# Hybrid decoder layer, float32, one core: projections of the MLP and of the embedding gate as 2x2 block products with seven multiplications

## The chip, the cores and the metric

The kernel runs on one core of a Trainium2 chip. The metric is device time of one execution in microseconds (us); the median of the runs is compared. Its engines are TensorE (PE; its weight loads are listed as PEld), VectorE (DVE), ScalarE (ACT), GpSimd (POOL) and SyncE (SP, which here only issues DMAs).

## The reference, cut to what matters

One layer: four token mixers (S5, forgetting attention, RWKV-7, stick-breaking attention), a gated merge with output projection and layer norm, then the part that is changed. x is 1024 tokens by 1024 channels, all float32.

```python
merged = sum(jax.nn.sigmoid(gates[:, :, n]) * (branches[n] @ w_branch[i, n]) for n in range(4))
h1 = _layer_norm(DEEPNORM_ALPHA * h + merged @ w_out[i], ln1_g[i], ln1_b[i])
up = jnp.square(jax.nn.relu(h1 @ mlp_w1[i]))                 # 1024 x 4096, squared ReLU
ple = jax.nn.sigmoid(h1 @ ple_gate_w[i]) * (p[i] @ ple_w[i]) # gated embedding, p is 1024 x 256
h = _layer_norm(DEEPNORM_ALPHA * h1 + up @ mlp_w2[i] + ple, ln2_g[i], ln2_b[i])
```

(The names `h1`, `up` and `ple` are put in here for the text.)

## The kernel before, in words

Every large product is made of float32r matmuls of 128x128 weights by 128x512 values. For float32 accuracy each operand is split into a high part (ACT casts it) and a low part (DVE or POOL subtracts), and three matmuls take the place of one: high by high, high by low, low by high. A product over 1024 input channels for one 128x512 output is thus 8 x 3 = 24 matmuls in one PSUM bank (`dense`).

The program is written by a planner: `Driver` keeps a model of when each engine and each value is free, Python generators yield at each step, and PE's order is the order in which their matmuls are emitted. On DVE and ACT the instructions are sorted by the start times of that model (end of `body`); SP and POOL issue in the order of emission. The planner has a cost for each instruction (`Timed.cost`, `T.matmul`); it has none for two engines that get in each other's way.

Weights come as 128x512 float32 tiles `wr` (SP), are split into `wh` and `wl`, and wait there for PE (`WStream`). Stages:

- The mixers and the merge, to about 1012 us.
- `out_proj`: eight blocks of 128 tokens, 48 matmuls each. After each block `h1_block` does layer norm on DVE, PE turns the result (8 transposes), ACT writes h1 times alpha into the accumulators `acc` (tiles `mg`), ACT and DVE write the high and low parts `xh`, `xl`.
- `mlp`: four chunks of 1024 hidden channels. For each: eight up products in two token halves (`up`: ACT takes the ReLU out of PSUM, DVE squares, ACT and DVE split into `wo` tiles); then, for three chunks, eight down products (DVE adds each to `acc`). After the first chunk the gate and embedding products (`gated`). The hidden values never leave SBUF.
- The down product of the fourth chunk is done with tokens on the partitions (`begin`, `step`), so that the last layer norm (`finish`) reads PSUM directly.

In matmuls of 128x512: 384 in `out_proj`; 4 x 8 x 2 x 24 = 1536 up; 3 x 8 x 2 x 24 = 1152 down; 8 x 2 x 24 = 384 gate; 8 x 2 x 6 = 96 embedding; 384 in the last part.

Of the kernel before, what the change touches and what calls it, by code (L numbers as in the profile page):

```python
# [16 lines left out]
P = 128  # L17
S = 1024
# [296 lines left out]
def body(ctx, tc, I, O, dbg=None):  # L315
# [1315 lines left out]
    ypool = pool_in(ctx, name="yp", bufs=4)  # L1631
    tpool = pool_in(ctx, name="tp", bufs=2)
# [38 lines left out]
    ws.limit = len(items)  # L1671
# [8 lines left out]
    wo = pool_in(ctx, name="wo", bufs=16)  # L1680
# [10 lines left out]
    def wo_split(i):  # L1691
        p_ = (wot(), wot())
        split(*p_, wraw[i])
        if i == 6:
            ws.gate = len(items) - 7
        if i + 2 < 7:
            wo_load(i + 2)
        return p_
# [30 lines left out]
    def h1_block(tb, xr):  # L1729
# [3 lines left out]
        for d4 in range(2):  # L1733
# [3 lines left out]
            for j in range(4):  # L1737
                i = d4 * 4 + j
                src = o[:, j * P:(j + 1) * P]
                A.copy(xh[i][:, sl], src)  # L1740
                A.activation(out=acc[i][:, sl], in_=src, func=AF.Copy, scale=ALPHA)
            for j in range(4):
                i = d4 * 4 + j
                V.tensor_tensor(out=xl[i][:, sl], in0=o[:, j * P:(j + 1) * P], in1=xh[i][:, sl].bitcast(F32), op=ALU.subtract)
# [17 lines left out]

    def mlp():
        yield from out_proj()
        for c in range(4):
            hid = []

            def up(w, a, b, h, last):
                hs = slice(h * 512, (h + 1) * 512)
                while tdone[0] < 4 * h + 4:  # L1770
                    yield "wait"
                o = yield from dense(w, KT, xh, xl, h * 512, last=last)
                rl = tpool.tile([P, 512], F32, tag="th", name=nm("rl"))
                A.activation(out=rl, in_=o, func=AF.Relu)
                V.tensor_tensor(out=rl, in0=rl, in1=rl, op=ALU.mult)
                split(a[:, hs], b[:, hs], rl)
            if c == 0:
                hid += [(wot(), wot()) for _ in range(2)]
                for h in range(2):
                    for f in range(2):  # L1780
                        yield from up(ws.get(), *hid[f], h, True)
            for f in range(len(hid), 8):
                w = ws.get()
                hid.append((wot(), wot()))
                for h in range(2):
                    yield from up(w, *hid[f], h, h == 1)
            hh, hl = [a for a, _ in hid], [b for _, b in hid]
            if c < 3:
                for dt_ in range(8):
                    w = ws.get()  # L1790
                    for h in range(2):
                        hs = slice(h * 512, (h + 1) * 512)
                        o = yield from dense(w, KT, hh, hl, h * 512, last=h == 1)
                        V.tensor_tensor(out=acc[dt_][:, hs], in0=acc[dt_][:, hs], in1=o, op=ALU.add)
            else:
                ws.gate = len(items)
                w2 = []

                def begin(tb):
                    outs[tb] = [pmm() if (tb * 2 + h) % 8 < 3 else px() for h in range(2)]  # L1800
                    for j in range(8):
                        T.turned(outs[tb][j // 4][:, j % 4 * P:j % 4 * P + P], acc[j][:, tb * P:(tb + 1) * P], j % 4 == 0)

                def step(tb, h, kt):
                    sl, hs = slice(tb * P, (tb + 1) * P), slice(h * 512, (h + 1) * 512)
                    if kt == len(w2):
                        w2.append(ws.dst[ws.get()])
                    for a, b in ((hh, 0), (hh, 1), (hl, 0)):
                        T.matmul(outs[tb][h], lhsT=a[kt][:, sl], rhs=w2[kt][b][:, hs], start=False, stop=kt == 7 and a is hl)
                for tb in range(3):  # L1810
# [121 lines left out]
```

## Time and profile before

| | |
|---|---|
| median of 3 runs | 1927.45 us (1927.32 to 1929.45) |
| the profiled execution | 1929.31 us, span 1927.5 us |
| instructions in the profile | 26665, of them 10035 matmuls |
| busy: PE, PEld, DVE, ACT, POOL | 98%, 80%, 54%, 33%, 5% |
| mean granted clock of TensorE | 0.988 of full speed |
| moved by DMA | 155.62 MB, mean 81 GB/s |

The span is what the profiler saw between the first and the last instruction; 1.8 us of the execution's own time lie around it. A busy PE is a PE with a matmul in its pipeline: matmuls overlap (one lasts about 0.39 us and the next starts 0.23 us after it), so PE's rate is read from starts, not from durations.

### The profile page before, as it was taken

How to read it: one execution, taken by the hardware profiler on the slowest of the kernel's cores; microseconds unless marked ns; L12 is line 12 of the kernel's file. 1: busy time of each engine (PE TensorE's matmuls, PEld its weight loads, DVE VectorE, ACT ScalarE, POOL GpSimd, SP SyncE). 2: the span in 40 equal slices, each digit the busy share in tenths (PEclk: the TensorE clock that was granted, in tenths of full speed). 3: DMA queues.
4: the chain of work that ended last, by engine and by line, in shares of the span. 5: the costliest groups of instructions: out<-in, count | busy, mean ns of one | idle time of the engine just before them, and what ended most of it. 6: DMA issues, size and time to landing. Idle time of an engine off the chain costs nothing.

```text
span 1927.5 us, 26665 instructions
## 1 busy us (share of the span) xinstructions
PE 1889.2 (98%) x10035; PEld 1546.2 (80%) x10035; DVE 1049.2 (54%) x2312; ACT 635.7 (33%) x1324; POOL 95.1 (5%) x151
## 2 busy tenths in 40 slices
PE   8999999999999999999999999999999999999998
PEld 7877777768788877778778888888888888888886
DVE  8775755527786763888686643233333233223454
ACT  5443342225453214555443242122132123113310
POOL 0331111100000000000000000000000000000000
PEclk9999999999999979999999999999999999999999
DMA  6343322215422314122452121121111111111211
GB/s 248 116 123 94 90 75 86 87 55 155 144 62 81 91 49 122 61 62 62 153 161 85 33 66 46 53 68 45 52 49 50 47 53 44 54 45 50 86 68 55
DMA packets 111888, 155.62 MB, mean 81 GB/s; under 512 B 30592, under 2 KB 51360, under 8 KB 111632
## 3 DMA queue, kind: packets, MB, share of 16 engines
q1 hardware_dynamic: 107872, 140.31, 23.3%
q0 software_dynamic: 3888, 13.62, 2.1%
q8 instruction: 79, 1.29, 0.3%
q14 instruction: 49, 0.40, 0.1%
HBM read 127.40 MB, written 26.48 MB: 80 GB/s over the span
## 4 chain that ended last, share of the span: by engine, by line
PE 66%; DVE 5%; DMA 1%; issue 1%; ACT 1%; DVEq 0%; ACTq 0%; SPq 0%
PE mm L325 57%; PE x L325 8%; DVE R L278 2%; PE x L330 2%; DVE W L278 1%; DVE tq L278 1%; DMA wr<-in_w_in_dram 1%; DVE Z L278 0%; ACT W L278 0%; ACT R L278 0%; DVE th L278 0%; DMA th<-scr_g 0%; PE x L335 0%; DMA st<-scr_qk 0%; DVE WR L278 0%
## 5 line engine op out<-in xcount | busy, mean ns | idle before, releaser
L325 PE MATMUL mm<-t,wh 128*128 128x512 f32 x2880 | 906.8, 396 | 3.4 <-ACT th L278 2.2
L325 PEld LDWEIGHTS mm<-t,wh 128*128 128x128 f32 x2880 | 532.9, 189 | 115.3 <-ACT th L278 2.6
L325 PE MATMUL mm<-t,wl 128*128 128x512 f32 x1440 | 563.3, 391 | 0.8 <-DVE wl L278 0.7
L325 PEld LDWEIGHTS mm<-t,wl 128*128 128x128 f32 x1440 | 271.4, 189 | 59.8 <-DVE wl L278 1.6
L278 ACT CAST wh<-wr 128x512 fp32r<-128x512 f32 (+1 forms) x257 | 156.8, 611 | 445.2 <-PE mm L325 410.6
L278 DVE TENSOR_TENSOR wl<-wr,wh 128x512 fp32r<-128x512 f32 (+1 forms) x207 | 138.5, 671 | 268.4 <-ACT wh L278 265.7
L325 PE MATMUL mm<-wo,wh 128*128 128x512 f32 x768 | 236.5, 389 | 0.0
L325 PEld LDWEIGHTS mm<-wo,wh 128*128 128x128 f32 x768 | 144.1, 188 | 30.0
L325 PE MATMUL mm<-wo,wl 128*128 128x512 f32 x384 | 149.4, 389 | 0.0
L278 DVE TENSOR_TENSOR rl<-rl 128x512 f32<-128x512 f32 x64 | 44.1, 688 | 98.2 <-ACT rl L278 98.2
L325 PE MATMUL mm<-wo,t 128*128 128x512 f32 x384 | 89.0, 391 | 0.0
L325 PEld LDWEIGHTS mm<-wo,wl 128*128 128x128 f32 x384 | 72.1, 188 | 14.9
L325 PEld LDWEIGHTS mm<-wo,t 128*128 128x128 f32 x384 | 71.6, 188 | 14.5
L278 POOL TENSOR_TENSOR wl<-wr,wh 128x512 fp32r<-128x512 f32 x50 | 67.1, 1341 | 280.6 <-ACT wh L278 280.4
L278 DVE TENSOR_TENSOR mg<-mg,mm 128x512 f32<-128x512 f32 x48 | 32.8, 683 | 83.3 <-PE mm L325 83.3
L325 PE MATMUL mm<-y,vh 128*128 128x512 f32 x240 | 75.2, 395 | 0.0
L278 ACT ACTIVATE th<-mm 128x512 f32<-128x512 f32 x60 | 36.3, 606 | 111.9 <-PE mm L325 108.7
L278 ACT ACTIVATE rl<-mm 128x512 f32<-128x512 f32 x64 | 38.2, 597 | 105.1 <-PE mm L325 105.1
L278 DVE TENSOR_TENSOR wo<-rl,wo 128x512 fp32r<-128x512 f32 x64 | 44.4, 693 | 43.9 <-ACT wo L278 43.8
L278 DVE SCALAR_TENSOR_TENSOR th<-th,mm 128x512 f32<-128x512 f32 x64 | 43.6, 681 | 33.5 <-PE mm L325 31.7
L278 ACT CAST wo<-rl 128x512 fp32r<-128x512 f32 x64 | 39.7, 621 | 50.9 <-DVE rl L278 50.9
L278 ACT CAST PTh<-x 128x512 fp32r<-128x512 f32 (+1 forms) x96 | 43.0, 483 | 39.8 <-PE x L330 39.2
(339 smaller groups left out, 2483.7 us busy)
## 6 DMA issues: line engine op xcount, KB each, us to landing
wr<-in_mlp_w_dram SPq DMA_DIRECT2D x116, 256.0 KB
wr<-in_w_in_dram SPq DMA_DIRECT2D x110, 256.0 KB
st<-scr_qk SPq DMA_DIRECT2D x56, 128.0 KB
scr_qk<-st SPq DMA_DIRECT2D x20, 256.0 KB
scr_g<-gs SPq DMA_DIRECT2D x20, 256.0 KB
wr<-in_w_branch_dram SPq DMA_DIRECT2D x40, 128.0 KB
th<-scr_g SPq DMA_DIRECT2D x20, 256.0 KB
xr<-in_xT_dram SPq DMA_DIRECT2D x16, 256.0 KB
```

Source lines behind the costliest of these rows:

```text
L278: r = f(*a, **kw)
L325: return nc.tensor.matmul(out, lhsT=lhsT, rhs=rhs, **kw)
L330: return nc.tensor.transpose(out, in_, idn)
```

## The change

The planner's cost of a matmul is altered. The up products, the gate and the first three chunks of the down product are now done in groups. A group multiplies a 256x1024 block of weights by 1024x1024 values, both seen as 2x2 blocks: weights A11..A22 of 128x512, values B11..B22 of 512 channels by 512 tokens. Instead of eight block products there are seven, of 12 matmuls each, with sums of weights (S1 to S4) and of values (T1 to T4). Part of the adding is done by letting a PSUM bank go on accumulating after it was read (`BANKS`).

- POOL makes the four sums of weights per group; ACT and DVE split seven tiles of weights per group into `wp` pairs.
- The values of an up or gate group are made from h1 once (`operands_h1`). The low part of the last of each four tiles is made by POOL, the others by DVE.
- An up group takes its four blocks out of PSUM (three copies on ACT, three additions on DVE), applies squared ReLU, makes T1 to T4 on DVE, and stores seven 128x512 tiles to DRAM (`scr_H`). All 16 up groups and the 4 gate groups come first; then three times four down groups. `operands_hidden` loads the seven value operands of a chunk (28 tiles) and splits them again.
- The fourth chunk's hidden values go to DRAM (`scr_H3`) and come back for the last part.
- The embedding product is done in two halves beside `h1_block`, and stored to DRAM (`scr_B`); the gate groups load it.
- `yp`, `tp` and `wo` are now in a stack of pools, `mid`, that is closed after `out_proj`; pool `sp` (tiles `wp`, `sx`, `sn`) takes its place, and pool `fin` follows `sp` for the last part.

```diff
-            drv.tensor((max(n, 2 * m) if rhs.dtype == F32R else 4 * max(n, m)) / 2380.0, out, [lhsT, rhs], not kw["start"])
+            drv.tensor((max(n + m // 4, 2 * m) if rhs.dtype == F32R else 4 * max(n, m)) / 2400.0, out, [lhsT, rhs], not kw["start"])
...
-                A.copy(xh[i][:, sl], src)
-                A.activation(out=acc[i][:, sl], in_=src, func=AF.Copy, scale=ALPHA)
...
-                V.tensor_tensor(out=xl[i][:, sl], in0=o[:, j * P:(j + 1) * P], in1=xh[i][:, sl].bitcast(F32), op=ALU.subtract)
+                if j % 2:
+                    V.tensor_copy(acc[i][:, sl], o[:, j * P:(j + 1) * P])
+                else:
+                    A.copy(acc[i][:, sl], o[:, j * P:(j + 1) * P])
...
+    B_OPS = ("B11", "B21", "T2", "T1", "T3", "B22", "T4")
+    A_OPS = ("A11", "A12", "S2", "S1", "S3", "S4", "A22")
+    BANKS = "XYXZXZX"
+    NPAIR, NSN = 5, 8
+    GROUPS = [g for c in range(4) for g in (("U", c, 0), ("U", c, 1), ("P", 0, c), ("U", c, 2), ("U", c, 3))]
+    GROUPS += [("D", c, i) for c in range(3) for i in range(4)]
...
+        def paired(g, name, frees):
+            src = raws[g, name]
+            while (1, 5) not in fed_units or live["pair"] >= NPAIR or drv.ready(src) > drv.now:
+                yield None
+            live["pair"] += 1
+            h, l = pair_of(sp().tile([P, 1024], F32R, tag="wp", name=nm("wp"), bufs=NPAIR))
+            split(h, l, src)
...
+            added(g, "S1", r("A21"), r("A22"), ALU.add)
+            added(g, "S2", r("S1"), r("A11"), ALU.subtract)
+            added(g, "S3", r("A11"), r("A21"), ALU.subtract)
+            added(g, "S4", r("A12"), r("S2"), ALU.subtract)
...
+    def operand(ph, n, src):
+        t = operand_tile(n)
+        h, l = pair_of(t)
+        A.copy(h, src)
+        (G if len(phases[ph].get(n, ())) == 3 else V).tensor_tensor(out=l, in0=src, in1=h.bitcast(F32), op=ALU.subtract)
...
+    def operands_hidden(c):
+        jobs = [(n, kt) for n in B_OPS for kt in range(4)]
...
+                while len(loads) < min(len(jobs), k + 4) and live["sn"] < NSN:
+                    m, j = jobs[len(loads)]
+                    loads.append(sn())
+                    SY.dma_start(out=loads[-1], in_=SCR["H"][c * 4 + j, H_ROW[m]])
...
+    def blocks_of(take):
+        kept = {}
+        def ev(n, o):
+            if n in (0, 2, 3):
+                kept[n] = sn()
+                A.copy(kept[n], o)
+            elif n == 6:
+                take("21", o)
+            else:
+                t = kept.pop({1: 0, 4: 3, 5: 2}[n])
+                V.tensor_tensor(out=t, in0=o, in1=t, op=ALU.add)
+                take({1: "11", 4: "22", 5: "12"}[n], t)
...
+    def down_blocks(i):
+        def ev(n, o):
+            a, h = {0: (0, 0), 1: (0, 0), 2: (0, 1), 3: (1, 1), 4: (1, 1), 5: (0, 1), 6: (1, 0)}[n]
+            t = acc[2 * i + a][:, h * 512:(h + 1) * 512]
+            V.tensor_tensor(out=t, in0=t, in1=o, op=ALU.add)
...
+        for n, (bank, a, x) in enumerate(zip(BANKS, A_OPS, B_OPS)):
...
+            for kt in range(4):
...
+                T.matmul(o, lhsT=h[:, ks], rhs=t[:, 0:512], start=new and kt == 0, stop=False, skip_group_check=not new)
+                T.matmul(o, lhsT=h[:, ks], rhs=t[:, 512:1024], start=False, stop=False, skip_group_check=not new)
+                T.matmul(o, lhsT=l[:, ks], rhs=t[:, 0:512], start=False, stop=kt == 3, skip_group_check=not new)
...
+        yield from ple_half(0, stage0)
+        fed_units["half"] = True
+        while tdone[0] < 8:
+            yield "wait"
+        mid.close()
+        late["stack"] = ctx.enter_context(ExitStack())
+        late["sp"] = pool_in(late["stack"], name="sp", bufs=1)
+        drv.add(fetch_raw(), 2)
+        drv.add(make_pairs(), 2)
+        drv.add(operands_h1(), 3)
...
+        yield from ple_half(1, stage1)
...
+        for g, after in zip(GROUPS, GROUPS[1:] + [None]):
+            end = after is None or phase_of(after) != phase_of(g)
+            if end and after is not None:
+                drv.add(operands_hidden(after[1]), 2)
+            yield from group(g, end)
```

How the instructions move, at three places. The first is POOL's program after the output projection. Before, POOL has only DMA issues there (`y` are the rows of x, `t` the parameters of the last norm):

```order
L278 DMA y_11324<-in_x_dram 128x1024
L278 DMA y_11431<-in_x_dram 128x1024
L278 DMA t_16497<-in_ln_g_dram 128x1024
L278 DMA t_16498<-in_ln_b_dram 128x1024
L1928 UNCONDITIONAL_BRANCH
```

Now it goes on like this (`mg` is h1, `sn` the plain sums of values, `t` and `sx` low parts of operands, `ws` sums of weights from `wr`):

```order
L278 TENSOR_TENSOR sn_11673<-mg_4377,sn_11673 128x512
L278 TENSOR_TENSOR sn_11729<-mg_4375,mg_4371 128x512
L278 TENSOR_TENSOR ws_11758<-wr_11657,wr_11691 128x512
L278 TENSOR_TENSOR ws_11762<-wr_11621,wr_11657 128x512
L278 TENSOR_TENSOR ws_11760<-ws_11758,wr_11621 128x512
L278 TENSOR_TENSOR t_11722<-sn_11719,t_11722 128x512
L278 TENSOR_TENSOR t_11725<-sn_11718,t_11725 128x512
L278 TENSOR_TENSOR sn_11719<-mg_4378,sn_11719 128x512
L278 TENSOR_TENSOR ws_11764<-wr_11623,ws_11760 128x512
L278 TENSOR_TENSOR sn_11775<-mg_4376,mg_4372 128x512
```

From the first operand to the last one of h1, `sx_11899`, POOL has 19 such rows; in the whole program 164 more than before, each a tensor_tensor that reads two SBUF tiles.

The second place is ACT between the two halves of the embedding product. Before, ACT's rows after the output projection split weights and h1 (`xh` is `t`), none of them waiting for a pool:

```order
L278 CAST wh_11574<-wr_10640 128x512
L278 CAST wh_11592<-wr_10659 128x512
L278 ACTIVATE rl_11598<-mm_11542 128x512
L278 CAST t_104<-x_11613 128x128
L278 ACTIVATE mg_4368<-x_11613 128x128
```

Now, after the last value of the first half (`pb_11557`), come the first tiles of pool `sp`, `wp_11573`, and between them and `wp_11611`, which the second half's first matmul needs, seven operand casts:

```order
L278 ACTIVATE pb_11557<-mm_11550 128x512
L278 CAST t_11566<-mg_4371 128x512
L278 CAST wp_11573<-wr_11481 128x512
L278 CAST wp_11578<-wr_11525 128x512
L278 CAST t_11583<-mg_4372 128x512
L278 CAST t_11586<-mg_4373 128x512
L278 CAST t_11589<-mg_4374 128x512
L278 CAST t_11592<-mg_4375 128x512
L278 CAST t_11595<-mg_4376 128x512
L278 CAST t_11598<-mg_4377 128x512
L278 CAST t_11601<-mg_4378 128x512
L278 CAST wp_11611<-wr_11569 128x512
```

The store of `pb_11557` to DRAM must have landed before `wp_11573` may be written, since `sp` lies on the memory of `mid`.

The third place is DVE where one down chunk follows another. Before, a down product has two splits of weights and two additions for 48 matmuls:

```order
L278 TENSOR_TENSOR wl_12311<-wr_12182,wh_12310 128x512
L278 TENSOR_TENSOR wl_12329<-wr_12200,wh_12328 128x512
L278 TENSOR_TENSOR mg_4369<-mg_4369,mm_12297 128x512
L278 TENSOR_TENSOR mg_4370<-mg_4370,mm_12335 128x512
L278 TENSOR_TENSOR wl_12375<-wr_12250,wh_12374 128x512
```

Now, in the last group of the first down chunk (`t` are the low parts of the next chunk's operands, `wp` those of weights):

```order
L278 TENSOR_TENSOR mg_4377<-mg_4377,x_15379 128x512
L278 TENSOR_TENSOR wp_15411<-ws_15338,wp_15411 128x512
L278 TENSOR_TENSOR t_15417<-sn_15383,t_15417 128x512
L278 TENSOR_TENSOR t_15425<-sn_15385,t_15425 128x512
L278 TENSOR_TENSOR mg_4377<-mg_4377,x_15404 128x512
L278 TENSOR_TENSOR wp_15434<-wr_15291,wp_15434 128x512
L278 TENSOR_TENSOR t_15437<-sn_15387,t_15437 128x512
L278 TENSOR_TENSOR mg_4377<-mg_4377,x_15379 128x512
L278 TENSOR_TENSOR wp_15463<-wr_15344,wp_15463 128x512
L278 TENSOR_TENSOR t_15466<-sn_15420,t_15466 128x512
```

From `t_15417` to the last of the 28 operands DVE has 42 such rows, 21 operands, 10 splits of weights and 11 additions, and POOL has 15.

## Rows read from the trace of the kernel before

**Rows 1.** The page: span, busy time of each engine, share of the span, instructions.
```profile
span 1927.5 us, 26665 instructions
PE 1889.2 (98%) x10035; PEld 1546.2 (80%) x10035; DVE 1049.2 (54%) x2312; ACT 635.7 (33%) x1324; POOL 95.1 (5%) x151
```
**Rows 2.** The stretches of the program (mixers and merge; output projection; up, gate and down; last part; tail): us, then busy time and instructions of PE, PEld, DVE, ACT, POOL, granted clock, DMA share, GB/s.
```profile
0.00:1012.50 1012.50, 982.43 (x5971) 794.31 (x5972) 694.05 (x1648) 423.57 (x868) 89.16 (x140) 0.98 0.34 104
1012.50:1105.90 93.40, 93.40 (x443) 77.93 (x442) 63.84 (x174) 26.98 (x129) 4.88 (x10) 1.00 0.19 60
1105.90:1824.80 718.90, 718.90 (x3177) 595.34 (x3176) 241.22 (x374) 173.93 (x305) 0.41 (x1) 1.00 0.16 52
1824.80:1919.00 94.20, 94.20 (x449) 78.65 (x447) 45.60 (x106) 10.98 (x22) 0.64 (x2) 1.00 0.21 73
1919.00:1927.50 8.50, 0.29 (x2) 0.00 (x0) 4.50 (x12) 0.20 (x1) 0.00 (x0) 0.77 0.16 62
```
**Rows 3.** PE in order of time at the start of the output projection, and at the end of it: start, us, instruction (merged).
```profile
1012.58 18.53 PE L325 MATMUL mm<-wo,t 128*128 128x512 f32 x81
1030.94 1.03 PE L330 MATMUL x<-cst,y 128*128 128x128 f32 x8
...
1113.36 1.03 PE L330 MATMUL x<-cst,y 128*128 128x128 f32 x8
1114.14 0.71 PE L325 MATMUL mm<-t,wh 128*128 128x512 f32 x2
```
**Rows 4.** Splits of four tiles in a row on ACT and on DVE, at the start of the last part: start, us, instruction, idle time before it and who ended it; and what follows them on ACT.
```profile
1826.99 2.18 ACT L278 CAST t<-wr 128x512 fp32r<-128x512 f32 x4
1832.02 1.24 ACT L278 CAST t<-wr 128x512 fp32r<-128x512 f32 x2 [2.85 <-DMA wr<-in_mlp_w2t_dram]
1834.07 1.26 ACT L278 CAST t<-wr 128x512 fp32r<-128x512 f32 x2 [0.81 <-DMA wr<-in_mlp_w2t_dram]
1836.48 0.62 ACT L278 CAST t<-wr 128x512 fp32r<-128x512 f32 x1 [1.14 <-DMA wr<-in_mlp_w2t_dram]
```
```profile
1827.72 2.49 DVE L278 TENSOR_TENSOR t<-wr,t 128x512 fp32r<-128x512 f32 x4
```
**Rows 5.** POOL's subtractions of 128x512, as a group: shortest, median, longest in ns.
```profile
L278 POOL TENSOR_TENSOR wl<-wr,wh x50: 1263/1290/1785, 46.2 to 394.4; 128x512 fp32r<-128x512 f32 x50
```
**Rows 6.** DVE and POOL at the same time, three places: start, us, instruction.
```profile
189.93 1.27 POOL L278 TENSOR_TENSOR wl<-wr,wh 128x512 fp32r<-128x512 f32 x1 [11.95 <-ACT wh L278]
...
209.05 1.28 POOL L278 TENSOR_TENSOR wl<-wr,wh 128x512 fp32r<-128x512 f32 x1 [11.61 <-ACT wh L278]
...
108.73 1.29 POOL L278 TENSOR_TENSOR wl<-wr,wh 128x512 fp32r<-128x512 f32 x1 [1.04 <-ACT wh L278]
```
```profile
189.68 0.36 DVE L278 TENSOR_TENSOR tp<-L,Tn 128x192 f32<-128x192 f32 x1
190.07 1.33 DVE L278 TENSOR_TENSOR Tn<-Tn,tp 128x192 f32<-128x192 f32 x1
...
208.85 0.27 DVE L278 TENSOR_TENSOR tp<-L,Tn 128x120 f32<-128x120 f32 x1
209.16 1.32 DVE L278 TENSOR_TENSOR Tn<-Tn,tp 128x120 f32<-128x120 f32 x1
...
109.27 0.75 DVE L278 SCALAR_TENSOR_TENSOR xo<-mm,vec,xo 128x511 f32<-128x511 f32 x1 [4.57 <-ACT xo L278]
```
**Rows 7.** The layer norm of the last block of tokens on DVE, first and last row, and what follows it.
```profile
1106.07 0.69 DVE L278 SCALAR_TENSOR_TENSOR y<-y,mm 128x512 f32<-128x512 f32 x1
...
1110.84 1.41 DVE L278 SCALAR_TENSOR_TENSOR y<-y,rs,y 128x512 f32<-128x512 f32 x2
1112.16 1.29 DVE L278 TENSOR_TENSOR wl<-wr,wh 128x512 fp32r<-128x512 f32 x2
```
**Rows 8.** A store from SBUF to DRAM: issues, KB each, median us from issue to landing.
```profile
scr_v<-vs POOLq DMA_DIRECT2D x8, 128.0 KB, 2.0
```
**Rows 9.** Granted clock (after POOL's busy time) around two pauses of PE; columns as in rows 2.
```profile
420.00:425.00 5.00, 3.11 (x16) 2.26 (x14) 3.71 (x8) 2.55 (x5) 0.00 (x0) 1.00 0.15 52
425.00:430.00 5.00, 2.12 (x7) 1.92 (x8) 2.64 (x9) 0.96 (x2) 0.00 (x0) 0.52 0.30 105
430.00:435.00 5.00, 5.00 (x19) 4.04 (x18) 1.38 (x3) 0.00 (x0) 0.50 (x1) 0.80 0.15 52
...
670.00:675.00 5.00, 4.21 (x20) 3.30 (x18) 4.93 (x6) 0.60 (x1) 0.00 (x0) 1.00 0.00 0
675.00:680.00 5.00, 4.41 (x20) 3.51 (x20) 2.33 (x4) 0.00 (x0) 0.00 (x0) 0.77 0.09 26
680.00:685.00 5.00, 5.00 (x17) 3.65 (x17) 1.80 (x3) 1.23 (x2) 0.00 (x0) 0.50 0.00 0
685.00:690.00 5.00, 5.00 (x15) 3.87 (x15) 1.44 (x3) 1.69 (x4) 0.00 (x0) 0.50 0.00 0
690.00:695.00 5.00, 5.00 (x36) 3.96 (x36) 2.69 (x6) 0.35 (x1) 0.00 (x0) 0.86 0.56 135
```
**Rows 10.** A stretch in which the DMA engines were full; columns as in rows 2.
```profile
440.00:445.00 5.00, 5.00 (x23) 4.14 (x23) 3.37 (x6) 3.28 (x7) 0.00 (x0) 1.00 1.01 301
```

More of the change, by code (lines that the diff above doesn't have):

```diff
@@ L1669, in merged @@
                                op1=ALU.subtract)
-    ws.limit = len(items)
+    ws.limit = last0
     fill = merges()
@@ L1694, in wo_split @@
         if i == 6:
-            ws.gate = len(items) - 7
+            ws.gate = last0 - 1
         if i + 2 < 7:
@@ new lines, in drop, with fetch_raw @@
+    def drop(what):
+        live[what] -= 1
+    def fetch_raw():
+        for g in GROUPS:
+            w1, w2 = sources(g)
+            for name, src, c in (("A11", w1, 0), ("A12", w1, 512), ("A21", w2, 0), ("A22", w2, 512)):
+                while live["raw"] >= NRAW or fed_units.get("loads", 0) < 12:
+                    yield None
+                live["raw"] += 1
+                raws[g, name] = t = wpool.tile([P, 512], F32, tag="wr", name=nm("wr"), bufs=NRAW)
+                SY.dma_start(out=t, in_=src[:, c:c + 512])
+        fed[0] = 1
@@ new lines, in operands_hidden @@
+    def operands_hidden(c):
+        jobs = [(n, kt) for n in B_OPS for kt in range(4)]
+        loads = []
+        for k, (n, kt) in enumerate(jobs):
+            while True:
+                while len(loads) < min(len(jobs), k + 4) and live["sn"] < NSN:
+                    m, j = jobs[len(loads)]
+                    loads.append(sn())
+                    SY.dma_start(out=loads[-1], in_=SCR["H"][c * 4 + j, H_ROW[m]])
+                if k < len(loads) and n in freed[c] and drv.ready(loads[k]) <= drv.now:
+                    break
+                yield None
+            yield from operand(c + 1, n, loads[k])
+            drop("sn")
@@ new lines, in ple_half @@
+    def ple_half(h, stage):
+        for dt_ in range(8):
+            k = 2 + dt_ // 2
+            while (h, k) not in fed_units:
+                yield "wait"
+            o = pmm()
+            for kt in range(2):
+                xa, xb = fed_units[h, kt]
+                ks = slice(dt_ % 2 * 256 + kt * P, dt_ % 2 * 256 + kt * P + P)
+                a, b = (x[:, ks] for x in fed_units[h, k])
+                T.matmul(o, lhsT=a, rhs=xa, start=kt == 0, stop=False)
+                T.matmul(o, lhsT=a, rhs=xb, start=False, stop=False)
+                T.matmul(o, lhsT=b, rhs=xa, start=False, stop=kt == 1)
+                yield
+            if dt_ % 2:
+                used_units.add((h, k))
+                if h:
+                    live["pair"] -= 1 + 2 * (dt_ == 7)
+            t, out = stage(dt_)
+            A.activation(out=t, in_=o, func=AF.Copy, scale=0.5)
+            if out is not None:
+                SY.dma_start(out=out[0], in_=out[1])
@@ L1763, in mlp @@
     def mlp():
+        drv.add(ple_feed(), 2)
         yield from out_proj()
[L1765 to L1778, printed above, removed]
[L1779 to L1835 removed]
@@ new lines, in mlp, with begin, step @@
+        late["stack"].close()
+        late["fin"] = pool_in(ctx, name="fin", bufs=1)
+        ws.gate = len(items)
+        hid, w2 = [], []
+        def begin(tb):
+            outs[tb] = [pmm() if (tb * 2 + h) % 8 < 3 else px() for h in range(2)]
+            for j in range(8):
+                T.turned(outs[tb][j // 4][:, j % 4 * P:j % 4 * P + P], acc[j][:, tb * P:(tb + 1) * P], j % 4 == 0)
+        def step(tb, h, kt):
+            sl, hs = slice(tb * P, (tb + 1) * P), slice(h * 512, (h + 1) * 512)
+            if kt == len(w2):
+                hid.append(ws.dst[ws.get()])
+                w2.append(ws.dst[ws.get()])
+            for a, b in ((0, 0), (0, 1), (1, 0)):
+                T.matmul(outs[tb][h], lhsT=hid[kt][a][:, sl], rhs=w2[kt][b][:, hs], start=False, stop=kt == 7 and a == 1)
```

264 lines of the change are left out of this document (225 added, 39 removed).

## The prediction

> **What bounds the kernel now.** I read the page's busy times first, then the windows by stage, then PE in order of time, and last the other engines at the places where the change gives them work. PE is busy for 98% of the span, POOL for 5% [rows 1]. By stage PE idles only in the mixers: 1012.5 − 982.4 = 30 us. From 1012.5 to 1919 it is busy all the time at a granted clock of 1.00 [rows 2]. In the up, gate and down stage, 718.9 us long, DVE is busy for 241 us and POOL for 0.4. So PE's rate is the bound there: 81 matmuls in a row start over 1030.94 − 1012.58 = 18.36 us, 0.2267 us each [rows 3], and the stage's 1536 + 384 + 96 + 1152 = 3168 matmuls times 0.2267 are 718.2 us of its 718.9. A matmul taken away there is time taken away, as long as the others keep up.
>
> **What is removed.** Up, gate and down are 3072 matmuls; 32 groups of 7 products of 12 make 2688. Embedding, output projection and last part keep theirs. 384 × 0.2267 = **−87.0 us**.
>
> **What steady groups add.** A group lasts 84 × 0.2267 = 19.0 us on PE. In an up group DVE has 18 rows. A tensor_tensor of 128x512 takes 1.29 for two [rows 7] and 2.49 for four [rows 4], so 0.60 to 0.62 each; I take 0.61: 11.0 us. POOL has four sums of weights at a median of 1.29 [rows 5], 5.2 us. The two do not run side by side. A DVE op that needs 0.36 takes 1.33 when a POOL op runs, and one of 0.27 takes 1.32: 0.97 and 1.05 lost. One that reads PSUM is not held (0.75 beside POOL) [rows 6]. Four POOL ops at 0.97 add 3.9: 14.9 of 19.0 us. ACT has 11 rows at (2.18 − 0.62) / 3 = 0.52 [rows 4], under 6 us. Cost 0, hidden behind PE; the cover on DVE is 4 us per group.
>
> **The first transition** (t0 is the end of the output projection). Without waits, PE has half an embedding product (48 matmuls, 10.9), 8 transposes (0.8 [rows 3]), the other half (10.9) and six products (16.3) before the seventh product needs the last operand of h1: t0 + 38.9. Now the waits. The last layer norm keeps DVE until 1112.25, t0 + 6.4 [rows 7], and one split of weights queues behind it (t0 + 7.0), where PE has already waited some 1.3 us. The first half then ends at t0 + 13.0, is taken out of PSUM (0.6) and stored, which takes 2.0 [rows 8]: only at some t0 + 16 may the first tile of the new pool be written. ACT then makes ten casts in order (0.52 each) up to `wp_11611`, t0 + 21.2, its low part at t0 + 22; until there the second half cannot start, so PE idles for some 9 us. Meanwhile DVE starts at t0 + 16.5 on the 44 rows that end with the last low part, 44 × 0.61 = 26.8, and meets POOL's 19 rows, 19 × 0.97 = 18.4: t0 + 61.7. Against 38.9 that is **+23**. Bounds: with no loss beside POOL, PE's own 22 + 10.9 + 16.3 = 49.2, so +10; with each POOL row costing its whole 1.29, 67.8, so +29. I take 23, since the loss was measured.
>
> **Three chunk boundaries.** The operands of a chunk need loads of hidden values that earlier products still write or that share slots with them, so DVE's 42 rows (25.6 us) and POOL's 15 must pass within about 13 products, 35.4 us, of which 2.7 go before the first load lands: 32.6. Eleven of the 42 rows add from PSUM and are not held, so of 15 × 0.97 = 14.6 I count 74%, 10.8: 25.6 + 10.8 = 36.4, 4 us late each, **+12** for three. Bounds: 0, if POOL's ops mostly fall on those additions; and 25.6 + 15 × 1.29 = 45.0, 12.3 late each, 37.
>
> **A rule against it.** By the Trainium skill, SBUF — State Buffer, section Who interferes with whom, a DVE instruction with two SBUF inputs and a GpSimd instruction that reads SBUF exclude each other, and the loser waits for the whole instruction. The trace agrees in kind, and that a DVE op with one SBUF input escapes. By that rule a POOL op that comes first costs DVE all its 1.29 instead of 0.97: rival C below.
>
> **The last part.** Its hidden values now come from DRAM, so a step of 18 matmuls (4.08 us) needs four tiles, two before. Four casts are 2.1, and after four ACT waited 2.85 for the next load [rows 4]: 4.9 per step, 0.8 short over eight steps, 6.4 at most from that; loads made ahead cover about half. I take 3, and 1 for the last addition on DVE ahead of the transposes: **+4**, between 1 and 9.
>
> **The clock.** After a pause of a few us the granted clock stood at 0.52 and 0.80 for ten us, and once at 0.50 for over ten us after a pause of 1.4 among small matmuls [rows 9]. The two pauses of the first transition (about 9 us, and the one at the seventh product) may each cost some 2 us beyond their length: **+4**, between 0 and 14 (two times 7: rows 9 show 0.50 for ten us, 5 us lost, and 0.77 and 0.86 in the five before and behind, 2 us).
>
> **The mixers.** The planner's new cost of a matmul reorders PE there without adding any: 0, within ±10, a third of the 30 us of idle time that stands there [rows 2].
>
> **The sum.** −87 + 23 + 12 + 4 + 4 = −44. The profiled execution took 1929.3, so 1885.3; the median lies 1.9 below it: **1884 us**.
>
> **Rivals.**
> - A, the meeting of DVE and POOL costs little: PE's own path of 49 us holds at the first transition (+10), boundaries are free, last part +4, clock +2: −71, 1856. For it: POOL often waits for its own inputs. Against it: both cases in the trace lose nearly the whole op [rows 6]. Chance 0.20.
> - B, slower than before: DVE's queue in order becomes the bound of the steady groups. A product's bank must be read within about one product, 2.72 us, and an addition behind one held op (1.33) and two others (1.2) comes at that edge. Each late reading then stops PE, in 20 up and gate groups. It turns the sign when the 20 groups lose 44 us, 2.2 us each; at 2.5 us each, 20 × 2.5 = 50: 1934. For it: in-order queue, no cost for the two engines' exclusion in the planner. Against it: 15 of 19 us, and even at 0.69 (the longest DVE op of this kind [rows 7]) and 1.29 it is 12.4 + 5.2 = 17.6. Chance 0.08.
> - C, POOL's op costs DVE its full 1.29 everywhere: first transition 29, boundaries 25.6 + 0.74 × 19.4 − 32.6 = 7.3 each, 22 for three; steady groups 16.2, still hidden. −87 + 29 + 22 + 4 + 4 = −28: 1899. For it: with both queues full, every POOL op starts right behind a DVE op. Against it: rows 6 lose 0.3 less. Chance 0.10.
> - D, loads bind at the boundaries: 28 operands and some 8 weights of 256 KB in 35.4 us are 267 GB/s, and the DMA engines were full at 301 [rows 10], while SP issues them in order behind stores. At 8 us more for each boundary, +24: 1908. Chance 0.08.
> - E, the mixers' order costs 15 us: 1899. Chance 0.05.
> - That the change doesn't do what it says: PE's program has 384 matmuls fewer, of the same shape. The gain could only vanish if they started every 0.259 us (0.2267 × 3072 / 2688) instead of 0.2267; nothing in their form says so. That way lies in B.
>
> **How the numbers follow.** The forecast has 0.49. It and A span 1856 to 1899; the bounds of the first transition (10 and 29), the boundaries (0 and 37) and the clock could add, best to −87 + 10 + 0 + 1 + 0 = −76, 1851. With C, D and E on the upper side the range is 1852 to 1915; B and the far ends are left out. About 0.2% (3.9 us) is what a measurement can tell from no change. Faster by more than that: A, forecast, C, D and E, less a little of their tails, 0.91. Slower: most of B, 0.07. Within: 0.02.
>
> **What would show it.** Right: 9651 matmuls at 0.227 us between starts inside products; PE pauses of 5 to 10 us right after the output projection, ended by ACT or by a store's landing, and one of 10 to 15 before the first seventh product, ended by DVE or POOL; DVE's subtractions over 1 us beside POOL; 3 to 6 us at each of the three boundaries; none inside up groups; POOL busy some 200 us longer (164 rows). Wrong: PE waits of over 0.5 us between products of steady groups (B), waits for DMAs at boundaries (D), or PE's idle time before 1012 changed by over 10 us (E). If the first transition costs 10 with POOL's ops overlapping DVE's at their normal durations, the step on their exclusion was wrong (A).

## The result, and the profile after

The changed kernel takes 1951.05 us (median of 4 runs, 1947.94 to 1956.22), the kernel before, run beside it, 1928.45. The ratio is 1.0119, 95% interval 1.0095 to 1.0143: **slower by 1.2%**. Forecast were 1884 us, in a range of 1852 to 1915. The profiled execution took 1951.2 us.

The page's busy times of the changed kernel, which answer to [rows 1]:

```profile
span 1949.1 us, 27154 instructions
PE 1831.1 (94%) x9651; PEld 1486.4 (76%) x9651; DVE 1307.9 (67%) x2560; ACT 710.3 (36%) x1410; POOL 347.4 (18%) x315
```

PE has its 384 matmuls less and is busy for 58 us less, but the span is 21.6 us longer: PE now idles for 118 us, before for 38. Where, the windows by stage tell (columns as in [rows 2]: mixers and merge; output projection; up, gate and down in four pieces, cut where the second embedding half ends and inside the groups; last part):

```profile
0.00:1040.40 1040.40, 988.04 (x5971) 801.20 (x5972) 687.38 (x1645) 417.77 (x864) 87.22 (x140) 0.97 0.32 101
1040.40:1133.70 93.30, 93.30 (x442) 77.94 (x441) 61.45 (x149) 15.81 (x49) 4.87 (x10) 1.00 0.18 63
1133.70:1174.30 40.60, 25.73 (x105) 19.81 (x105) 28.55 (x45) 21.86 (x43) 8.07 (x5) 0.83 0.45 142
1174.30:1280.14 105.84, 91.14 (x373) 71.44 (x372) 81.24 (x90) 38.12 (x68) 47.50 (x31) 0.95 0.35 119
1280.14:1553.72 273.58, 268.32 (x1178) 220.42 (x1176) 194.44 (x246) 90.20 (x164) 87.79 (x56) 1.00 0.40 135
1553.72:1844.80 291.08, 268.90 (x1141) 217.28 (x1140) 194.84 (x254) 108.76 (x191) 110.80 (x73) 0.97 0.42 135
1844.80:1941.00 96.20, 95.66 (x449) 78.31 (x447) 55.98 (x122) 17.58 (x33) 1.09 (x2) 1.00 0.33 115
```

The mixers, in which not one instruction of PE was added, end 1040.4 − 1012.5 = 27.9 us later. The output projection takes its 93.3 us as before. Up, gate and down take 711.1 us where 718.9 − 87.0 = 631.9 would have been the whole gain. The last part and the tail take 1.7 us more. Inside the groups I read the losses from the starts of the fourth product of each group, which are 84 × 0.2267 = 19.04 us apart when PE waits for nothing. They sum up so (t0 is the end of the output projection):

| us lost against PE's own pace | forecast | measured |
|---|---|---|
| mixers | 0 | 27.9 |
| first transition, up to the second group's fourth product (at t0 + 49.8 without waits) | 23, and 4 of clock | 32.7 |
| three gate groups and the groups behind them | 0 | 13.6 |
| three chunk boundaries, clock included | 12 | 32.7 |
| last part and tail | 4 | 1.7 |
| 384 matmuls less | −87.0 | −87.0 |
| sum | −44 | +21.6 |

Of the 79 us that the up, gate and down stage loses, 62 are 29 waits of PE. The other 17 are matmuls behind those waits that started more than 0.2267 us apart, where the granted clock was below 1.00. The forecast had 4 for the clock, at the first transition alone.

In steady groups PE really keeps 19.04 us: 17 of the 31 distances between groups are 19.04, 4 more 19.3. The time is lost at few places. The PE timeline (start, us, instruction, idle time before it and who ended it) shows them; first the first transition, then one gate group, then the first and the second boundary:

```profile
1158.09 1.22 PE L325 MATMUL mm<-wp,wp 128*128 128x512 f32 x2 [11.11 <-ACT wp L278]
1161.83 9.81 PE L325 MATMUL mm<-wp,wp 128*128 128x512 f32 x36 [2.52 <-DVE wp L278]
1180.05 3.03 PE L325 MATMUL x<-t,wp 128*128 128x512 f32 x12 [2.41 <-DVE wp L278]
1189.89 1.22 PE L325 MATMUL mm<-t,wp 128*128 128x512 f32 x2 [3.89 <-ACT wp L278]
...
1249.32 7.38 PE L325 MATMUL x<-t,wp 128*128 128x512 f32 x24 [2.07 <-DVE wp L278]
1258.42 2.57 PE L325 MATMUL x<-t,wp 128*128 128x512 f32 x10 [1.72 <-DVE wp L278]
...
1606.28 0.96 PE L325 MATMUL mm<-sx,wp 128*128 128x512 f32 x3 [2.40 <-DVE sx L278]
...
1696.50 1.22 PE L325 MATMUL mm<-sx,wp 128*128 128x512 f32 x2 [5.46 <-POOL sx L278]
```

The 36 matmuls at 1161.83 take 9.81 us; 36 at [rows 3]'s pace and 0.2 for the last one's end are 8.3. The 1.5 us more are the clock's price: PE had idled 11.1 and 2.5 us just before, and the granted clock of these 9.81 us is 0.85 (0.54 in the first 3.2, near the lower of its two levels, 1.2 GHz of 2.4, then 1.00). The forecast had this in kind for the first transition. It had nothing of the kind behind the boundaries, where the second one shows 0.62 (windows as above):

```profile
1161.83:1171.64 9.81, 9.81 (x36) 7.73 (x36) 8.97 (x11) 6.27 (x12) 3.29 (x2) 0.85 0.56 186
1696.50:1702.00 5.50, 5.50 (x16) 4.40 (x17) 1.97 (x4) 0.70 (x2) 1.18 (x1) 0.62 0.80 278
```

At the gate group DVE meets POOL's four sums of weights (DVE, then POOL):

```profile
1244.72 1.18 DVE L278 SCALAR_TENSOR_TENSOR sn<-sn,sn 128x512 f32<-128x512 f32 x1
1245.93 1.66 DVE L278 SCALAR_TENSOR_TENSOR mg<-mg,sn 128x512 f32<-128x512 f32 x1
1247.52 1.75 DVE L278 TENSOR_TENSOR wp<-wr,wp 128x512 fp32r<-128x512 f32 x1
1249.19 1.77 DVE L278 SCALAR_TENSOR_TENSOR sn<-sn,sn 128x512 f32<-128x512 f32 x1
1250.99 0.69 DVE L278 SCALAR_TENSOR_TENSOR mg<-mg,sn 128x512 f32<-128x512 f32 x1
```
```profile
1244.05 3.00 POOL L278 TENSOR_TENSOR ws<-wr,wr 128x512 f32<-128x512 f32 x2 [13.71 <-DMA wr<-in_mlp_w_dram]
1247.01 1.71 POOL L278 TENSOR_TENSOR ws<-ws,wr 128x512 f32<-128x512 f32 x1
1248.80 1.61 POOL L278 TENSOR_TENSOR ws<-wr,ws 128x512 f32<-128x512 f32 x1
```

Four DVE ops that take 0.69 alone take 1.18 to 1.77, and POOL's, 1.29 in [rows 5], take 1.5 to 1.7: they go by turns. The `wp` among them is the one that PE waits for at 1249.32. The wait at 1258.42 is of another kind. POOL has ended by then; the split that PE needs starts at 1257.68 and stands in DVE's order behind the reading of a bank (1256.34), for which DVE had waited 2.34 us because PE was late. At the second boundary the last operand hangs on another chain (POOL, then SP's queue):

```profile
1688.18 4.49 POOL L278 TENSOR_TENSOR ws<-wr,wr 128x512 f32<-128x512 f32 x2 [7.31 <-DMA wr<-in_mlp_w_dram]
1692.63 1.25 POOL L278 TENSOR_TENSOR ws<-ws,wr 128x512 f32<-128x512 f32 x1
1693.97 1.26 POOL L278 TENSOR_TENSOR ws<-wr,ws 128x512 f32<-128x512 f32 x1
1695.19 2.50 POOL L278 TENSOR_TENSOR sx<-sn,sx 128x512 fp32r<-128x512 f32 x2
```
```profile
1669.98 14.20 SPq L278 DMA_DIRECT2D sn<-scr_H  x15
1684.46 0.33 SPq L278 DMA_DIRECT2D wr<-in_mlp_w_dram  x1
```

SP issues the next group's weight load behind 15 loads of hidden values. POOL's sums wait for it, and the low part `sx`, whose inputs have long been there, stands behind those sums in POOL's order. PE waits 5.46 us for it, while DVE has done its last operand and idles.

### The profile page after: what moved, and what is told of

It is laid out like the page before. It is cut to its first block, busy times and chain, and to the rows that moved or that the text cites. A ratio compares the mean times of both kernels' runs of the same rounds, so it can differ in the third digit from the quotient of the medians.

```text
span 1949.1 us, 27154 instructions
## 1 busy us (share of the span) xinstructions
PE 1831.1 (94%) x9651; PEld 1486.4 (76%) x9651; DVE 1307.9 (67%) x2560; ACT 710.3 (36%) x1410; POOL 347.4 (18%) x315
## 4 chain that ended last, share of the span: by engine, by line
PE 75%; DVE 14%; issue 3%; DMA 3%; ACT 2%; POOL 2%; SPq 0%; DVEq 0%; ACTq 0%; POOLq 0%
PE mm L325 39%; PE x L325 33%; DVE R L278 2%; PE x L330 2%; POOL ws L278 1%; DVE wp L278 1%; DVE W L278 1%; DVE sn L278 1%; DVE t L278 1%; DVE tq L278 1%; DVE Tn L278 1%; DVE mg L278 1%; DVE sx L278 1%; DVE xo L278 1%; DMA sn<-scr_H 1%
## 5 line engine op out<-in xcount | busy, mean ns | idle before, releaser
L325 PE MATMUL mm<-t,wh 128*128 128x512 f32 x1600 | 514.4, 403 | 3.3 <-ACT wh L278 1.9
L325 PEld LDWEIGHTS mm<-t,wh 128*128 128x128 f32 x1600 | 295.1, 191 | 64.9 <-issue 2.9
L325 PE MATMUL mm<-t,wl 128*128 128x512 f32 x800 | 316.3, 395 | 8.4 <-DVE wl L278 8.4
L325 PE MATMUL x<-t,wp 128*128 128x512 f32 x1152 | 274.2, 395 | 15.5 <-DVE wp L278 12.4
L325 PEld LDWEIGHTS x<-t,wp 128*128 128x128 f32 x1152 | 217.4, 190 | 67.0 <-DVE wp L278 17.9
L325 PE MATMUL x<-sx,wp 128*128 128x512 f32 x768 | 189.1, 396 | 7.5 <-DVE mg L278 3.6
L325 PEld LDWEIGHTS mm<-t,wl 128*128 128x128 f32 x800 | 152.4, 191 | 42.9 <-DVE wl L278 9.7
L325 PEld LDWEIGHTS x<-sx,wp 128*128 128x128 f32 x768 | 146.2, 191 | 41.6 <-issue 5.7
L278 POOL TENSOR_TENSOR ws<-wr,wr 128x512 f32<-128x512 f32 x64 | 97.5, 1544 | 342.9 <-DMA wr<-in_mlp_w_dram 218.4
L278 DVE TENSOR_TENSOR wp<-wr,wp 128x512 fp32r<-128x512 f32 x102 | 97.7, 964 | 36.6 <-ACT wp L278 36.6
L325 PEld LDWEIGHTS mm<-sx,wp 128*128 128x128 f32 x384 | 72.3, 190 | 31.4 <-POOL sx L278 12.4
```

Source lines behind the costliest of these rows:

```text
L278: r = f(*a, **kw)
```

## The experiments

Two theories stood first: that the mixers' loss is the planner's new cost alone, and that POOL's work costs DVE more than it takes off it. Their rivals stand in each expectation. In the tables here "stage" is the time from the end of the output projection to the first transpose of the last part; ratios are to the kernel before, with 95% intervals.

### The cost in the planner alone, and the change without it

```diff
 # e1_cost: the kernel before, with
-  (max(n, 2 * m) if rhs.dtype == F32R else ...) / 2380.0
+  (max(n + m // 4, 2 * m) if rhs.dtype == F32R else ...) / 2400.0
 # e2_mixold: the changed kernel, with the old formula until out_proj begins, the new one from there
```

> The kernel before with one edit: the planner's new cost of a matmul. Nothing else of the change. Theory (the mixers lost 27.9 us, output projection from 1012.6 to 1040.5, because the new cost gives PE, DVE and ACT another order there): the output projection starts at about 1040, the stages behind it last as before, time 1928 + 28 = 1956. Rival (the mixers lost time through the rest of the change, say memory or DMAs laid out differently): starts at 1012 to 1016, time 1926 to 1932.

> The changed kernel with the planner's old cost of a matmul up to the output projection and the new one from there. Theory: PE's order in the mixers is that of before again, the output projection starts at 1012 to 1016, and the later stages keep their losses: 1951 - 28 = 1923, thus slightly faster than before. Rival (the rest of the change slows the mixers): 1945 to 1952.

e1: 1957.01 us (ratio 1.0165, 1.0137 to 1.0193). e2: 1927.94 (1.0009, 0.9992 to 1.0025). Forecast were 1956 and 1923. The windows of the mixers, first of e1, then of e2:

```profile
0.00:1040.90 1040.90, 991.11 (x5971) 803.07 (x5972) 689.18 (x1648) 419.26 (x866) 87.18 (x140) 0.97 0.32 101
```
```profile
0.00:1013.40 1013.40, 984.59 (x5971) 796.42 (x5972) 691.72 (x1645) 421.81 (x866) 90.22 (x140) 0.98 0.33 103
```

With the one edit the mixers of the kernel before last 1040.9 us, and without it those of the changed kernel 1013.4. The number of PE's instructions is the same in all four. Their order is the same in e1 as in the changed kernel, and in e2 as in the kernel before. e1's stage is 718.8 us, as before. So the planner's cost accounts for the whole loss of the mixers, and the rival is out. In e1, PE's idle time rises from 30.1 to 49.8 us, and its busy time by 8.7. No single wait explains it. These are PE's three largest waits in the mixers of e1, by what ended them (us in total, times, longest); in the kernel before, the first two stood at 4.8 and 1.8 us, and the third wasn't there:

```profile
PE x L330 <- DVE W L278: 9.8, 17, 1.3
PE mm L325 <- DVE wl L278: 8.1, 2, 4.1
PE x L325 <- DVE Tn L278: 6.2, 1, 6.2
```

### Other costs: is the new formula bad, or is any?

```diff
 # e9_cost2330, e10_cost2420: the kernel before, with
-  ... / 2380.0
+  ... / 2330.0      (e9)      / 2420.0      (e10)
```

> The kernel before with the divisor of the planner's matmul cost 2330 in place of 2380 (2% dearer), nothing else. PE's order in the mixers is again another. Theory (the order is sensitive and the shown one was a lucky or a tuned draw; any other costs time): output projection later than 1012 by 5 to 30 us, 1933 to 1958. Rival (the new formula itself is bad, a small change of the divisor is harmless): 1924 to 1931.

> The kernel before with the divisor 2420 in place of 2380 (1.7% cheaper), nothing else. As with 2330: by the theory of a sensitive order 1933 to 1958, by the rival 1924 to 1931.

e9: 1937.35 (1.0042, 1.0022 to 1.0062), the output projection starts at 1019.6. e10: 1928.05 (0.9999, 0.9975 to 1.0023), at 1012.0. With 2330 the theory's range held, with 2420 the rival's. Three other costs give three other orders, and these cost 9, 0 and 29 us. The order is sensitive, but not every change of it loses. The formula of the change charges (512 + 32) / 2400 = 0.2267 us for a large matmul, which is exactly the distance that [rows 3] shows; a truer price gave the worst order of the four.

### POOL's work moved to DVE

```diff
 # e4_allV: the changed kernel, in added(), operand() and operands_h1()
-  G.tensor_tensor(...)
+  V.tensor_tensor(...)
 # e6_allV_mixold: e4_allV and e2_mixold together
```

> The changed kernel with all of POOL's sums, differences and low parts from the output projection on moved to DVE (164 rows). Theory (a POOL op costs DVE more by locking it out, about 1.0 us, than DVE needs to do the work itself, 0.61 us, and it waits in POOL's order behind late loads): the first transition falls from 31 us lost to about 19, the three boundaries from 10.9 to 3 each, the waits at the gate groups from 15.6 to 4: 1951 - 12 - 24 - 11 = 1904, with no tensor op of POOL behind the mixers and DVE's subtractions of 128x512 all at 0.6 to 0.7. Rival (POOL's work beside DVE is a gain, the losses come from loads and order): 15 more rows x 0.61 = 9 us later at each boundary and 19 x 0.61 = 12 at the first transition, 1951 + 39 = 1990. Between: about 1950 if the losses are the loads' alone.

> Both edits: no work of POOL behind the mixers, and the old cost of a matmul up to the output projection. Theory: the two gains add, 1904 - 28 = 1876, faster than before by 52. Rival (one cause stands behind both, or DVE is the bound): 1950 or more.

e4: 1927.99 (1.0011, 0.9993 to 1.0029). e6: 1899.41 (0.9865, 0.9835 to 0.9894), **faster than the kernel before by 1.35%**. Alone each edit gains 23 us over the changed kernel, together they gain 52, so they add within what the intervals can tell. But moving POOL's work gains half of what was forecast, 23 us for 47. The windows of the stage, of e2 (POOL at work), then of e6 (POOL without work there):

```profile
1106.90:1817.20 710.30, 655.07 (x2793) 528.83 (x2792) 501.25 (x633) 258.66 (x465) 253.77 (x164) 0.97 0.39 133
```
```profile
1099.50:1787.60 688.10, 651.38 (x2794) 528.16 (x2793) 504.42 (x797) 258.10 (x465) 0.00 (x0) 0.98 0.41 137
```

This pair is the study's clearest. POOL worked for 254 us to take 164 rows off DVE, and saved DVE 504.4 − 501.3 = 3 us. At 0.60 each those rows are 98 us, so each POOL op took about 95 / 164 = 0.58 us of DVE's time away again. The losses by place:

| us lost | stage | first transition | gate groups | boundaries |
|---|---|---|---|---|
| e2: sums and low parts on POOL | 710.3 | 34.1 | 12.4 | 32.0 |
| e8: sums on POOL | 705.9 | 36.7 | 15.3 | 21.9 |
| e6: neither | 688.1 | 27.0 | 7.0 | 22.1 |

### Which of POOL's two jobs

```diff
 # e8_lowV: e2_mixold, and in operand()
-  (G if len(phases[ph].get(n, ())) == 3 else V).tensor_tensor(out=l, ...)
+  V.tensor_tensor(out=l, ...)
```

> The changed kernel with the old cost in the mixers (1928) and only the low parts of operands moved from POOL to DVE; POOL keeps the sums of weights and of h1. It tells which of POOL's two jobs cost the time that the move of both gave back (1928 to 1899). Theory (two jobs, two costs: low parts stand in POOL's order behind sums that wait for late weight loads, which stops PE 5.5 us at the second and third boundary; the sums hold DVE by excluding it, at the gate groups above all): waits of PE ended by POOL gone, boundaries from 10.9 to some 6 each, gate groups still 15: 1928 - 14 - 3 = 1911. Rival 1 (only the exclusion counts, by number of ops: 28 of 164): 1923. Rival 2 (low parts are all of it): 1900.

e8: 1918.07 (0.9947, 0.9926 to 0.9967), between the theory's 1911 and rival 1's 1923. In the profiled executions its stage is 4.4 us shorter than e2's; the medians lie 9.9 apart, and the runs don't show where the rest is. The table shows the theory's two costs: without POOL's low parts the boundaries fall from 32.0 to 21.9 and no wait of PE is ended by POOL any more; without the sums the first transition falls by 9.7 and the gate groups by 8.3. What the theory missed is that the first transition, where low parts were moved to DVE, loses 2.6 more than in e2. The gate groups lose 2.9 more too, though the edit moves nothing there. The changed kernel and e2, alike in this stage, differ there by 1.2 between their profiles; what the rest is isn't shown.

### Useless work on POOL

```diff
 # e12_idlepool: e7_pools (below), and in added()
   V.tensor_tensor(out=t, in0=a, in1=b, op=op)
+  for c in (0, 256):
+      G.tensor_tensor(out=spare[c // 256], in0=a[:, c:c + 256], in1=b[:, c:c + 256], op=op)
...
+  spare[:] = [wpool.tile([P, 256], F32, tag=tg, name=nm("idle"), bufs=1) for tg in ("vh", "vl")]
```

> The same version with useless work put on POOL: beside each of the 128 sums of weights on DVE, POOL adds the same two tiles in two halves into spare tiles that nobody reads. DVE and PE do what they did, and nobody waits for POOL's results. Theory (POOL's ops hold up DVE's ops with two SBUF inputs): DVE's busy time in the up, gate and down stage rises from 504 us by about 128 x 0.6 = 75 us with not one row more, and the places where DVE is late lose more, some 5 us at each boundary, 4 at the first transition, 2 at each gate group: 1899 + 25 = 1924. Rival (the losses of the changed kernel came only from waiting for POOL's results, in its own order): DVE's busy time stays at 504 and the time at 1899.

2000.21 us (1.0364, 1.0327 to 1.0400), 101 us over the same kernel without it. The window of the stage:

```profile
1109.90:1898.50 788.60, 692.20 (x2792) 545.90 (x2792) 593.75 (x797) 258.30 (x466) 274.59 (x256) 0.94 0.36 120
```

DVE has the same 797 rows as e6 and is busy 593.8 us, not 504: 89 us for 256 half ops, which is the theory's mechanism at about the theory's price (75 forecast). But the time rose four times as far as forecast. One steady up group shows why (DVE, POOL, PE; the first of the four sums stands just before these rows):

```profile
1278.94 0.69 DVE L278 TENSOR_TENSOR ws<-ws,wr 128x512 f32<-128x512 f32 x1
1279.55 1.22 DVE L278 TENSOR_TENSOR ws<-wr,wr 128x512 f32<-128x512 f32 x1
1280.70 1.22 DVE L278 TENSOR_TENSOR ws<-wr,ws 128x512 f32<-128x512 f32 x1
1281.84 1.22 DVE L278 TENSOR_TENSOR sn<-sn 128x512 f32<-128x512 f32 x1
1282.99 4.11 DVE L278 TENSOR_TENSOR sn<-sn,sn 128x512 f32<-128x512 f32 x4
1287.02 0.68 DVE L278 TENSOR_TENSOR wp<-ws,wp 128x512 fp32r<-128x512 f32 x1
```
```profile
1281.33 2.34 POOL L278 TENSOR_TENSOR idle<-wr,wr 128x256 f32<-128x256 f32 x2
1283.63 2.32 POOL L278 TENSOR_TENSOR idle<-wr,ws 128x256 f32<-128x256 f32 x2
```
```profile
1287.76 4.14 PE L334 MATMUL x<-t,wp 128*128 128x512 f32 x10 [2.09 <-DVE wp L278]
```

DVE's work in a group comes in one burst at its end: four sums, five rows on the hidden values, then the split that PE needs next. Held by turns, the burst ends after PE has run dry, although DVE idles later in the same group. PE waits 2.09 us, and then its ten matmuls take 4.14 us, at a granted clock of 0.59, where 2.4 would do. Most up groups took 22.8 to 23.6 us instead of 19.04. In the whole stage 69 of the 102 us that e12 lost against e7 are waits of PE, and 33 are matmuls started further apart than 0.2267 us; the forecast had nothing for the clock.

A rival cause is that POOL, which reads the weights too, hands their slots back later. It is not the main one: DVE waits only 0.7 us in all for loads of these weights (0.9 in e7), ACT and PE none. But SP waited 127 us in all for POOL before it issued a load, in e7 never, and loads of values stand behind these in SP's order. DVE's and ACT's waits for those rose by 7 and 10 us; how much of that reached PE isn't shown.

### The pool switch

```diff
 # e7_pools: e6_allV_mixold, and in mlp()
-  late["sp"] = pool_in(late["stack"], name="sp", bufs=1)
+  late["sp"] = Parts({tag: pool_in(late["stack"], name=tag, bufs=1) for tag in ("sn", "sx", "wp")})
+  late["sp"].parts["wp"].base = made      # made: the planner's time at the end of out_proj
```

> The version with nothing on POOL and the old cost in the mixers (1899), with pool sp split into three, so that the weight pairs wp lie on memory of the output projection's weights and no longer on that of the embedding values: the first cast into wp need not wait for the store of the last of those to land (3.5 us of ACT's time in the run before). Theory (PE's first pause, 10.6 us, is ACT's casts held by that store): first cast 3.5 to 4 us earlier, PE's pause about 7, the whole chain of DVE's operand rows as much earlier, 1899 - 4 = 1895. Rival (the pause is the weight loads', issued by SP once slots come free, or DVE's rows set the end of the first group anyway): 1898 to 1900.

1899.32 us (0.9839, 0.9805 to 0.9873), nothing gained over e6's 1899.41. Inside, the theory held. ACT's first casts into `wp`, of e6 (t0 = 1099.52) and of e7 (t0 = 1108.10):

```profile
1118.37 1.14 ACT L278 CAST wp<-wr 128x512 fp32r<-128x512 f32 x2 [3.48 <-DMA scr_B<-pb]
```
```profile
1123.52 1.14 ACT L278 CAST wp<-wr 128x512 fp32r<-128x512 f32 x2
```

They come at t0 + 15.4 in place of t0 + 18.9, PE's first pause is 7.2 us for 10.6, and the first transition costs 22.9 for 27.0. But of these 4.1 us the stage keeps 1.5: 0.5 are lost at the first gate group and 2.1 at the boundaries, and the total cannot show the rest: with one and the same order of the mixers, the output projection started anywhere from 1006.1 to 1016.4 in seven profiles.

### Fewer rows on DVE

```diff
 # e11_fewlows: e7_pools, and in operand(), group()
   A.copy(h, src)
+  if len(phases[ph].get(n, ())) < 3:
       V.tensor_tensor(out=l, ...)
...
-  T.matmul(o, lhsT=h[:, ks], rhs=t[:, 512:1024], ...)
+  T.matmul(o, lhsT=h[:, ks], rhs=xs[x][min(kt, 2)][:, 512:1024], ...)
```

> The version with nothing on POOL, the old cost in the mixers and the split pools (1899), with seven low parts of operands less on DVE in each of the four phases: the low part of the last of each four tiles is left out, and its matmuls read the low part of the third (so the output is less exact). ACT's casts, loads, PE's matmuls stay. Theory (at the first transition and at the boundaries DVE's rows, 0.60 us each, set the end): 7 x 0.6 = 4.2 us less at the first transition and at each boundary as far as they lose that much (about 23, 11, 5, 5 us lost now): 1899 - 4.2 - 4.2 - 4.2 - 4.2 = 1882. Rival (loads, ACT's casts or the hand-back of slots set the end): 1896 to 1900.

1889.93 us (0.9802, 0.9763 to 0.9840). The windows of the stage, of e7 and of e11:

```profile
1108.10:1794.70 686.60, 651.92 (x2794) 528.97 (x2793) 504.24 (x797) 258.21 (x465) 0.00 (x0) 0.98 0.40 137
```
```profile
1100.20:1772.90 672.70, 645.55 (x2794) 525.07 (x2793) 488.89 (x769) 258.32 (x466) 0.00 (x0) 0.98 0.42 140
```

With 28 rows less on DVE the stage is 13.9 us shorter, for 16.8 forecast. First transition −3.6; boundaries 13.0, 5.7 and 5.6 become 8.4, 2.7 and 2.7. So without POOL it is DVE's rows that set the end there. The window of the second boundary of e6 shows DVE full (34.4 of 35.0 us) while ACT and the DMA engines are not:

```profile
1612.00:1647.00 35.00, 32.06 (x135) 25.43 (x134) 34.41 (x57) 19.68 (x37) 0.00 (x0) 0.97 0.75 246
```

## Why the prediction was wrong

**Right.** The gain of 87.0 us is there: 9651 matmuls at the old pace, and whole groups at 19.04 us. The first transition cost 32.7 for 23 and 4 of clock, and it began as told: PE paused 11.1 us behind the store, ACT's casts and then DVE's rows. That DVE and POOL exclude each other was right, and e12 shows it by itself. A steady up group came out too: at 1299.18 DVE is busy 14.1 of 19.04 us, for 14.9 in the sum. The last part's 4 were 1.7.

**Near in size, not in form: the end of the first transition.** The forecast had one pause of 10 to 15 us before the first seventh product, ended by the last operand. The seventh product waited 1.79 us. The time went in eight short waits from the second half of the embedding product to the second group, 11.2 us in all. The longest, 3.89, stands before the fourth product: in ACT's order the cast of `wp` stood behind one that waited 6.41 us for a sum of POOL's.

**Wrong: "the mixers: 0, within ±10".** This one step carries 27.9 of the 66 us between forecast and result, and is the largest. (The sum itself is half a microsecond off: 1885.3 − 1.9 is 1883.4, not 1884.) I had bounded it by a third of the idle time that stood there, as if a new order could only shuffle existing waits. e1 shows that it made new ones: 20 us of idle time and 9 of busy time. Rival E named the place, at half the price, and its sign came: PE's idle time before the output projection rose from 30 to 52 us. But it isn't the whole miss: e2, without it, takes 1927.9 and is still 44 us above the forecast.

**Wrong: the boundaries, 12.** They cost 32.7. My sum of DVE's rows and POOL's exclusion left out POOL's own order: a low part behind sums, the sums behind a weight load, that load behind 15 others on SP. e8 takes POOL's low parts out and gives back 10. Most of the rest is DVE's pace: e6, with 57 DVE rows in 35 us and none on POOL, still loses 22, and e11 shows that these follow the number of DVE's rows. By my sum the 57 rows of e6 (42 and POOL's 15) would take 57 × 0.61 = 34.8 of 32.6 us, 2.2 late; e6 lost 5.4 and 5.6 at the second and third boundary and 11.1 at the first. So the window of 32.6 us was too generous; what shortens it, at the first boundary above all, isn't shown.

**Wrong: "steady groups: 0, hidden".** I compared sums, 14.9 of 19.0 us. For most groups it holds, but not at the gate groups, which I had not summed: 13.6. There DVE's work comes in a burst, and what counts is when the row that PE needs next ends, not how much of a group is idle. POOL's sums beside the burst are about half of it: e6, with the sums on DVE, still loses 7.0. Rival B's in-order queue was at work in three groups of twenty, not in all, and there more by late splits of weights than by late readings of banks; those stopped PE at the boundaries, 5.8 us in four waits.

**Too small: the clock, 4.** Matmuls that started further apart than 0.2267 us behind PE's waits cost 17 us in the stage. The forecast counted two pauses; there were 29.

**The price of a POOL op.** By the exclusion rule of the Trainium skill, SBUF — State Buffer, section Who interferes with whom, the loser waits for the whole instruction. The traces agree that the two take turns: in the gate group a DVE op beside POOL took up to 1.77 us, 1.08 over its 0.69. That is less than the whole of POOL's 1.29. On the average of 164 ops DVE lost 0.58 us, since not each POOL op met a DVE op with two SBUF inputs; the changed kernel's readings of PSUM beside POOL kept 0.68. Rival C, 1899 by that price, was not the way: its whole surcharge, 15 us, is smaller than the mixers' term.

None of the rivals alone explains why the result is slower than before. Undoing the two measured causes, the order of the mixers and POOL's work, gives 1899.4, between the forecast and the kernel before.

What stays open: why just that order of the mixers loses 28 us, since its waits are spread over many places; why the first boundary loses twice as much as the others without POOL; and how much of e12's surplus came by later loads.

## What to carry to other kernels

An edit to a planner's cost moves every stage that the planner writes; price it by building each half of the change alone, since a truer cost can give a worse order. Work given to POOL may not be taken off DVE where DVE's ops read two SBUF tiles: compare DVE's busy time with and without it before counting on it. And where work comes in bursts in step with PE, ask when the row that PE needs next ends, not what share of the group the engine is busy. Count the clock behind every pause that is left.

## What the runs showed of the hardware

- 164 POOL ops of 128x512 saved DVE 3 us of busy time in 504, where the moved rows are worth some 98.
- In the up, gate and down stage of the changed kernel, 162 DVE ops of 128x512 with both inputs in SBUF met a POOL op and lasted 1.29 us on average, 0.69 without one; 57 that read PSUM met one and kept 0.68.
- POOL's own sums became slower beside a busy DVE: 1.29 us in [rows 5], but these groups of the changed kernel (count, busy us, mean ns, idle time before and its ends) show 1.53 to 1.68:

```profile
L278 POOL TENSOR_TENSOR ws<-ws,wr 128x512 f32<-128x512 f32 x32 | 53.8, 1681 | 0.0
L278 POOL TENSOR_TENSOR ws<-wr,ws 128x512 f32<-128x512 f32 x32 | 49.0, 1531 | 2.4
```

- Halving a POOL op did not halve it under load: two ops of 128x256 took 2.3 us beside a busy DVE, one of 128x512 1.5 to 1.7, and every DVE op with two SBUF inputs meanwhile 1.15 between starts, not 0.60.
